# Down projection of 12 of 22 FFN pairs from seven block products, on one core of Trainium2

## The chip, the cores and the metric

One core of one Trainium2 chip runs the whole kernel; the other cores do nothing. The metric is device time in microseconds of one execution. TensorE multiplies matrices into PSUM; VectorE, ScalarE and GpSimd work element by element; SyncE, ScalarE and GpSimd issue transfers. Each engine runs its own instructions in order and waits for the others by semaphores.

## What is computed

An encoder block over 512 tokens of width 2048. The last part, which the change touches, is the channel mixing:

```python
h = modulate(layer_norm(x), shift2, scale2)
f = (jax.nn.silu(h @ w_ffn_gate[l]) * (h @ w_ffn_up[l])) @ w_ffn_down[l]
x = layer_norm_affine(DEEPNORM_ALPHA * x + gate2 * f, ln2_g[l], ln2_b[l])
```

The hidden width is 5632. All of it is float32.

## The kernel before

**Splits.** A float32 matrix is held as a high part (a cast to fp32r by ScalarE, line 95) and a low part (the rest, a subtraction by VectorE, line 96). `mm3` (lines 76 to 79) makes one float32 product out of three matmuls: high by high, high by low, low by high. So each product costs three matmuls, and each weight block needs one cast and one subtraction first. Split weights sit in four buffers each, `wh` and `wl`; raw weights in four buffers `raw` of 1024 elements by 128 partitions (512 KB).

**Pairs.** The hidden width is worked in 22 pairs of 256 rows. For each pair the gate product, SiLU, the up product and their product (`eg`, line 1138) give the pair's hidden values, 128 partitions by four blocks of 256, and `store_hid` (line 1016) writes them to `hid_d` in device memory from ScalarE's queue. Pairs 0 and 1 are made plainly. For pairs 2 to 21 the gate and up products are already made from seven block products in place of eight (`strassen`): a loop of four units, each with one load of 512 KB, `weight_sums` (three sums by GpSimd into `tt`, lines 1058 to 1060, and two splits, `hr`/`lr` and `wh`/`wl`), and 42 matmuls of 256 columns. `combine` (lines 1088 to 1092) adds the banks up on ScalarE and VectorE.

**Down projection.** It follows all the pairs. `down` takes four pairs at a time (0 to 3, 4 to 7, and so on to 19). `load_hid` (lines 1105 to 1111) loads a pair's hidden values and splits them into tiles that stay for the group (`A`, `M`, at the end `hh`, `hl`). Then, for each of four column chunks of 512 and each pair: one weight load of 512 KB, one split, and 4 token tiles x 2 row blocks x 3 matmuls of 512 columns. After each chunk four banks are drained by VectorE: multiplied by the gate row (`gate2`, line 1158) and added to the residual (lines 1161, 1163). The residual and the gate row come in with the first group on ScalarE's queue (lines 1151, 1153). Pairs 20 and 21 come last, in one stage with the final layer norm; their weights are multiplied by `gate2` on GpSimd and split during the last group (`load_last`, lines 1205 to 1213).

**Order.** The order within each engine is set by a scheduler of the language, from dependencies and the buffers that are free; the program's text gives the priorities. PSUM has eight banks, `ps_s` (4), `ps_g` (2), `ps_t` (2).

## Time and profile before

| | |
|---|---|
| median of 3 runs | 2667.24 us (2667.1 to 2670.86) |
| the profiled execution's own time | 2664.01 us |
| its span | 2662.0 us |
| TensorE busy | 2592.6 us (97%), 15563 matmuls recorded |
| VectorE, ScalarE, GpSimd busy | 1833.2, 1012.9, 1206.8 us (69%, 38%, 45%) |
| moved by DMA | 456.11 MB, 171 GB/s on average |

The profile is one execution, 3.2 us below the median of the timed runs. The gate and up products of pairs 2 to 21 lie at about 1330 to 2172 us of the span, the down projection at 2172 to 2608, the last two pairs and the final layer norm from there to the end. An engine's share of the whole span is a mean over stages with different limits, so the rows further down are taken by stage.

### The profile page before, as it was taken

What the parts mean: (1) busy time and instruction counts of PE and PEld (TensorE: products, weight loads), DVE (VectorE), ACT (ScalarE), POOL (GpSimd) and SP (SyncE); (2) the same over time, 40 slices, a digit from 0 to 9 for tenths busy, and PEclk for the clock granted to TensorE, in tenths of its full rate; (3) what the DMA queues carried; (4) which work ended last, traced back from release to release, by engine and by line L of the source; (5) the groups of instructions that cost most, each with busy time, mean ns of one, the idle gap of its engine ahead of it and who ended that gap; (6) DMA issues with size and microseconds to landing.
All of it is one profiled execution on the core that took longest, in us unless ns stands there. A gap on an engine that the chain in (4) does not pass through costs nothing. (4 is left out here: it accounts for less than half of the span.)

```text
span 2662.0 us, 40015 instructions
## 1 busy us (share of the span) xinstructions
PE 2592.6 (97%) x15563; PEld 2314.5 (87%) x15563; DVE 1833.2 (69%) x2244; ACT 1012.9 (38%) x1456; POOL 1206.8 (45%) x1033
## 2 busy tenths in 40 slices
PE   5999999999989999999899999999999999999998
PEld 4888888789878888888899999999999998888886
DVE  8886787874678644577777677777777755445566
ACT  3332433333344533346644443444444432212321
POOL 0008778876745011020368777776677720000023
PEclk8999999999999999999999999999999999999999
DMA  9976578775734444768753333333333364334442
GB/s 350 320 256 211 156 228 254 244 246 173 237 101 151 129 144 142 240 217 260 238 166 120 118 120 119 115 120 124 111 120 123 116 214 150 119 110 128 151 127 87
DMA packets 330798, 456.11 MB, mean 171 GB/s; under 512 B 19656, under 2 KB 208480, under 8 KB 330096
## 3 DMA queue, kind: packets, MB, share of 16 engines
q1 hardware_dynamic: 307840, 414.77, 49.3%
q10 hardware_dynamic: 22768, 38.78, 4.1%
q8 instruction: 122, 2.00, 0.3%
q14 instruction: 68, 0.56, 0.1%
HBM read 418.87 MB, written 34.62 MB: 170 GB/s over the span
## 5 line engine op out<-in xcount | busy, mean ns | idle before, releaser
L96 DVE TENSOR_TENSOR wl<-raw,wh 128x1024 fp32r<-128x1024 f32 (+2 forms) x342 | 446.7, 1310 | 323.0 <-ACT wh L95 321.6
L95 ACT CAST wh<-raw 128x1024 fp32r<-128x1024 f32 (+2 forms) x342 | 346.3, 1015 | 706.9 <-PE ps_s L79 270.7
L96 DVE TENSOR_TENSOR wl<-tt,wh 128x1024 fp32r<-128x1024 f32 x160 | 235.7, 1474 | 168.3 <-ACT wh L95 168.1
L1058 POOL TENSOR_TENSOR tt<-raw 128x512 f32<-128x512 f32 x160 | 244.2, 1527 | 190.7 <-DMA raw<-in_w_ffn_up_dram 70.0
L95 ACT CAST wh<-tt 128x1024 fp32r<-128x1024 f32 x160 | 167.7, 1049 | 309.4 <-PE ps_s L78 134.5
L1056 DVE TENSOR_TENSOR lr<-raw,hr 128x768 fp32r<-128x768 f32 x160 | 215.4, 1346 | 44.7 <-ACT hr L1055 44.0
L230 POOL TENSOR_TENSOR acc<-acc,tmp 128x512 f32<-128x512 f32 (+1 forms) x154 | 207.3, 1346 | 9.8
L1208 POOL TENSOR_TENSOR raw<-raw,gate 128x512 f32<-128x512 f32 x16 | 25.3, 1609 | 400.9 <-DMA raw<-in_w_ffn_down_dram 400.9
L1055 ACT CAST hr<-raw 128x768 fp32r<-128x768 f32 x160 | 133.6, 835 | 151.0 <-PE ps_s L78 71.4
L226 POOL TENSOR_SCALAR tmp<-braw,csil 128x512 f32<-128x512 f32 x112 | 136.3, 1218 | 117.8 <-DMA braw<-in_w_ada_dram 114.4
L1060 POOL TENSOR_TENSOR tt<-raw,tt 128x256 f32<-128x256 f32 x160 | 174.5, 1092 | 11.7
L1059 POOL TENSOR_TENSOR tt<-raw,tt 128x256 f32<-128x256 f32 x160 | 170.6, 1067 | 11.7
L77 PE MATMUL ps_g<-hTh,wh 128*128 128x512 f32 x384 | 152.1, 397 | 1.7 <-ACT wh L95 1.7
L79 PE MATMUL ps_g<-hTh,wl 128*128 128x512 f32 x384 | 151.0, 394 | 0.0
L78 PE MATMUL ps_g<-hTl,wh 128*128 128x512 f32 x384 | 150.4, 392 | 0.0
L220 DVE SCALAR_TENSOR_TENSOR acc<-braw,csil,acc 128x512 f32<-128x512 f32 x112 | 112.6, 1006 | 43.4 <-DMA braw<-in_w_ada_dram 42.5
L77 PE MATMUL ps_s<-wh,hTh 128*128 128x512 f32 (+1 forms) x384 | 138.1, 361 | 0.0
L77 PE MATMUL ps_s<-sh,wh 128*128 128x256 f32 x480 | 135.2, 282 | 2.7 <-ACT wh L95 2.7
L79 PE MATMUL ps_s<-sh,wl 128*128 128x256 f32 x480 | 136.2, 284 | 1.4 <-DVE wl L96 1.4
L78 PE MATMUL ps_s<-wl,hTh 128*128 128x512 f32 (+1 forms) x384 | 137.5, 358 | 0.0
L79 PE MATMUL ps_s<-wh,hTl 128*128 128x512 f32 (+1 forms) x384 | 137.2, 358 | 0.0
L78 PE MATMUL ps_s<-sl,wh 128*128 128x256 f32 x480 | 136.3, 284 | 0.0
(432 smaller groups left out, 8251.5 us busy)
## 6 DMA issues: line engine op xcount, KB each, us to landing
braw<-in_w_ada_dram SPq DMA_DIRECT2D x128, 512.0 KB, 4.3
raw<-in_w_in_dram SPq DMA_DIRECT2D x96, 512.0 KB, 5.0
raw<-in_w_ffn_gate_dram SPq DMA_DIRECT2D x96, 512.0 KB, 3.6
raw<-in_w_ffn_up_dram SPq DMA_DIRECT2D x96, 512.0 KB, 3.6
raw<-in_w_ffn_down_dram SPq DMA_DIRECT2D x88, 512.0 KB, 3.7
raw<-in_w_out_dram SPq DMA_DIRECT2D x64, 512.0 KB, 4.4
lraw<-in_w_ada_dram SPq DMA_DIRECT2D x56, 512.0 KB, 8.9
braw<-in_w_in_dram SPq DMA_DIRECT2D x24, 512.0 KB, 4.7
```

Source lines behind the costliest of these rows:

```text
L77: nc.tensor.matmul(ps, lhsT=ah, rhs=bh, start=start, stop=False)
L78: nc.tensor.matmul(ps, lhsT=ah, rhs=bl, start=False, stop=False)
L79: nc.tensor.matmul(ps, lhsT=al, rhs=bh, start=False, stop=stop)
L95: nc.scalar.copy(out=h[:, :n], in_=src)
L96: nc.vector.tensor_tensor(out=l[:, :n], in0=src, in1=h[:, :n], op=ALU.subtract)
L226: nc.gpsimd.tensor_scalar(out=dst[:, :n], in0=v[:, k, :], scalar1=col, scalar2=1.0, op0=ALU.mult, op1=ALU.mult)
L230: nc.gpsimd.tensor_tensor(out=acc2[:, :n], in0=acc2[:, :n], in1=dst[:, :n], op=ALU.add)
L1055: nc.scalar.copy(out=hr, in_=b[:, :, 1:4, :])
L1056: nc.vector.tensor_tensor(out=lr, in0=b[:, :, 1:4, :], in1=hr, op=ALU.subtract)
L1058: nc.gpsimd.tensor_tensor(out=t[:, :, 0:2, :], in0=b[:, :, 0:1, :].broadcast_to([P, 2, 2, P]), in1=b[:, :, 1:3, :], op=ALU.subtract)
L1059: nc.gpsimd.tensor_tensor(out=t[:, :, 2, :], in0=b[:, :, 2, :], in1=t[:, :, 0, :], op=ALU.subtract)
L1060: nc.gpsimd.tensor_tensor(out=t[:, :, 3, :], in0=b[:, :, 3, :], in1=t[:, :, 2, :], op=ALU.subtract)
```

## The change

Pairs 2 to 13 get their down projection from seven block products. Hidden values and weights are seen as 2 x 2 blocks (hidden: token halves by row blocks of the pair; weights: row blocks by halves of the 2048 columns).

- After the pair's product (line 1196 of the new file) `hidden_sums` makes four sums on GpSimd into `eu`. During the next pair's gate product the hook `pay` calls `store_parts` twice: it splits `eg` and `eu` (two more casts and subtractions of 1024) and stores the seven blocks that the products need, high and low, to `sets_d` from ScalarE's queue (line 1154), eight transfers of 0.13 or 0.26 MB a pair, 1.835 MB.
- The down projection of these 12 pairs is `strassen_down`: first three products for both column halves (`set1`, `weights1`), then four (`set2`, `weights2`). A unit is one pair and one column half: 18 or 24 matmuls of 512 columns. Weight sums are made on VectorE (lines 1174, 1175; 1226, 1227), then split as before. `need1` and `need2` (lines 1136, 1140) load the stored splits straight into a ring of 12 tiles, with no cast; `need2` of a pair is issued three units after its last use in the first set.
- Half tiles come by turns from `raw` (4) and `tp` (4 more). Sums stay in the accumulators `x2` without `gate2`; `convert` (lines 1268, 1269) multiplies by `gate2` and adds the residual, eight times, spread over the plain groups.
- Pairs 0, 1, 14 to 19 are done plainly in two groups of four, as before, 20 and 21 in the last stage. `load_last` multiplies in one GpSimd operation of 1024.

```diff
-    GROUP, N_LAST = 4, 2
+    GROUPS = [[2, 3, 4, 5, 6, 7, 8, 9, 10, 11, 12, 13]]
+    PLAIN = [[0, 1, 14, 15], [16, 17, 18, 19]]
+    N_LAST = 2
...
+    def need1(g):
+        tl = set1[g] = ring_tile((3, g))
+        nc.sync.dma_start(out=parts(tl).bitcast(F32)[:, :, 0:768], in_=sets_d[g][:, :, 1024:1792])
+
+    def need2(g):
+        tl = set2[g] = ring_tile((4, g))
+        nc.sync.dma_start(out=parts(tl).bitcast(F32), in_=sets_d[g][:, :, 0:1024])
+
+    def hidden_sums(g, eg, e):
+
+        nc.gpsimd.tensor_tensor(out=e[:, 0], in0=eg[:, 1], in1=eg[:, 2], op=ALU.subtract)
+        nc.gpsimd.tensor_tensor(out=e[:, 1], in0=e[:, 0], in1=eg[:, 3], op=ALU.subtract)
+        nc.gpsimd.tensor_tensor(out=e[:, 2], in0=eg[:, 3], in1=eg[:, 1], op=ALU.subtract)
+        nc.gpsimd.tensor_tensor(out=e[:, 3], in0=eg[:, 0], in1=e[:, 1], op=ALU.add)
+
+    def store_parts(g, v, moves):
+        for x, part in enumerate(split(v.rearrange("p b n -> p (b n)"), 1024)):
+            pb = part.bitcast(F32).rearrange("p (b n) -> p b n", b=4)
+            for to, b0, b1, st in moves:
+                n = (b1 - b0 + st - 1) // st
+                nc.scalar.dma_start(out=sets_d[g][:, x, to * 256:(to + n) * 256].rearrange("p (b n) -> p b n", b=n), in_=pb[:, b0:b1:st, :])
...
+    def weights1(g, c):
+        a, b = half_tile(), half_tile()
+        av, bv = a.rearrange("p (b n) -> p b n", b=2), b[:, :512]
+        nc.sync.dma_start(out=av, in_=w_rows(g, 0, c))
+        nc.sync.dma_start(out=bv, in_=w_rows(g, 1, c)[:, 1, :])
+        nc.vector.tensor_tensor(out=av[:, 1], in0=av[:, 1], in1=av[:, 0], op=ALU.add)
+        nc.vector.tensor_tensor(out=bv, in0=bv, in1=av[:, 1], op=ALU.add)
+        ah, al = split(a, 1024)
+        bh, bl = split(bv, 512)
+        return ((0, (ah[:, :512], al[:, :512])), (2, (bh[:, :512], bl[:, :512])), (1, (ah[:, 512:], al[:, 512:])))
...
-        bk = strassen(w_ffn_gate, 2 * g, "ssss")
+        bk = strassen(w_ffn_gate, 2 * g, "ssss", pay)
...
-        store_hid(g, eg)
...
+        if g in by_sums:
+            hidden_sums(g, eg, eu)
+            owed.append(lambda g=g, v=eg: store_parts(g, v, ((0, 0, 3, 2), (4, 3, 4, 1))))
+            owed.append(lambda g=g, v=eu: store_parts(g, v, ((2, 2, 4, 1), (5, 0, 2, 1))))
+        else:
+            store_hid(g, eg)
...
+    def weights2(g, c):
+        a, b = half_tile(), half_tile()
+        av, bv = a.rearrange("p (b n) -> p b n", b=2), b.rearrange("p (b n) -> p b n", b=2)
+        nc.sync.dma_start(out=bv, in_=w_rows(g, 0, c))
+        nc.sync.dma_start(out=av, in_=w_rows(g, 1, c))
+        nc.vector.tensor_tensor(out=bv, in0=bv, in1=av, op=ALU.add)
+        nc.vector.tensor_tensor(out=bv[:, 0], in0=bv[:, 0], in1=bv[:, 1], op=ALU.add)
+        ah, al = split(a, 1024)
+        bh, bl = split(b, 1024)
...
+    def products(pairs, sets, weights, c, step):
+        bk = None
+        for u, g in enumerate(pairs):
+            ws = ready.pop(0) if ready else weights(g, c)
+            if bk is None:
+                bk = [dbank() for _ in range(2 * len(ws))]
+            step(u, False)
+            for j, (b, w) in enumerate(ws):
+                for i in range(2):
+                    mm3(bk[2 * j + i], block(sets[g], b, i), w, u == 0, u == len(pairs) - 1)
+            step(u, True)
+        return bk
...
+    def convert(c, ts=range(NT)):
+        for t in ts:
+            zv = quad(x2[t], c)
+            xc = half_tile().rearrange("p (b n) -> p b n", b=2)
+            nc.sync.dma_start(out=xc, in_=quad(x2_d[t], c))
+            nc.vector.tensor_tensor(out=zv, in0=zv, in1=quad(gate2, c), op=ALU.mult)
+            nc.vector.scalar_tensor_tensor(out=zv, in0=xc, scalar=ALPHA, in1=zv, op0=ALU.mult, op1=ALU.add)
```

The order of the instructions changes at three places.

**ScalarE, end of an up product to the next gate product.** `eu<-ps_t` is the first step of the up product's `combine`; `hr` and `wh` are casts of the weights for the coming units. Before:

```order
L1088 COPY eu<-ps_t 128x256
L1055 CAST hr<-raw 128x768
L95 CAST wh<-tt 128x1024
L1055 CAST hr<-raw 128x768
L95 CAST wh<-tt 128x1024
L1016 DMA hid_d<-eg 128x1024
L1055 CAST hr<-raw 128x768
L95 CAST wh<-tt 128x1024
```

and now:

```order
L1089 COPY eu<-ps_t 128x256
L1056 CAST hr<-raw 128x768 x2
L95 CAST wh<-eg 128x1024
L95 CAST wh<-tt 128x1024
L1154 DMA sets_d<-wh 128x2x256
L1154 DMA sets_d<-wh 128x256
L1154 DMA sets_d<-wl 128x2x256
L1154 DMA sets_d<-wl 128x256
L95 CAST wh<-eu 128x1024
L1056 CAST hr<-raw 128x768
L1154 DMA sets_d<-wh 128x512 x2
L95 CAST wh<-tt 128x1024
```

The one store of `eg` gives way to two more casts and eight stores, and casts of weights stand between and behind these stores in the queue.

**SyncE, second half of the first product set** (before: the first group of the down projection). `raw` and `tp` are weight tiles; `Ah`, `Al` and their like are tiles of the ring, or before, of a group's hidden values. Before:

```order
L1108 DMA raw<-hid_d 128x1024 x2
L89 DMA raw<-in_w_ffn_down_dram 128x2x512 x16
L1108 DMA raw<-hid_d 128x1024 x4
L89 DMA raw<-in_w_ffn_down_dram 128x2x512 x16
L1108 DMA raw<-hid_d 128x1024 x4
```

and now:

```order
L1173 DMA raw<-in_w_ffn_down_dram 128x512
L1140 DMA Ah_23001<-sets_d 128x2x1024
L1172 DMA tp<-in_w_ffn_down_dram 128x2x512
L1140 DMA Al_23035<-sets_d 128x2x1024
L1173 DMA raw<-in_w_ffn_down_dram 128x512
L1172 DMA tp<-in_w_ffn_down_dram 128x2x512
L1173 DMA raw<-in_w_ffn_down_dram 128x512
L1140 DMA Ah_23069<-sets_d 128x2x1024
L1172 DMA tp<-in_w_ffn_down_dram 128x2x512
L1173 DMA raw<-in_w_ffn_down_dram 128x512
L1140 DMA Al_23103<-sets_d 128x2x1024
```

A weight load of 512 KB per 24 matmuls becomes two loads of 512 and 256 KB per 18, with one load of a pair's stored splits (line 1140) between them.

**VectorE, between the column halves of the second product set** (before: between two chunks of a group). `ps_g`, `ps_t`, `ps_s` are banks that are drained, `x_0` to `x_3` the accumulators. Before:

```order
L96 TENSOR_TENSOR wl<-raw,wh 128x1024 x4
L1158 TENSOR_TENSOR dtmp<-ps_s,gate_22227 128x512 x2
L1163 TENSOR_TENSOR x_0_22220<-x_0_22220,dtmp 128x512
L1163 TENSOR_TENSOR x_1_22221<-x_1_22221,dtmp 128x512
L1158 TENSOR_TENSOR dtmp<-ps_s,gate_22227 128x512 x2
L1163 TENSOR_TENSOR x_2_22222<-x_2_22222,dtmp 128x512
L1163 TENSOR_TENSOR x_3_22223<-x_3_22223,dtmp 128x512
L96 TENSOR_TENSOR wl<-raw,wh 128x1024 x4
```

and now:

```order
L1226 TENSOR_TENSOR raw<-raw,tp 128x1024
L1261 TENSOR_TENSOR x_0_22467<-ps_g,x_0_22467 128x512
L96 TENSOR_TENSOR wl<-raw,wh 128x1024
L1261 TENSOR_TENSOR x_1_22468<-ps_g,x_1_22468 128x512
L1261 TENSOR_TENSOR x_0_22467<-ps_t,x_0_22467 128x512
L1227 TENSOR_TENSOR raw<-raw 128x512
L1261 TENSOR_TENSOR x_1_22468<-ps_t,x_1_22468 128x512
L1261 TENSOR_TENSOR x_2_22469<-ps_s,x_2_22469 128x512
L1324 TENSOR_TENSOR x_2_22469<-x_2_22469,ps_s 128x512
L96 TENSOR_TENSOR wl<-tp,wh 128x1024
L1261 TENSOR_TENSOR x_3_22470<-ps_s,x_3_22470 128x512
L1324 TENSOR_TENSOR x_3_22470<-x_3_22470,ps_s 128x512
```

Four drains of two operations and a split of weights per unit become drains of one operation each, between the sums (lines 1226, 1227) and two splits of every unit; multiplications by `gate2` (line 1268) follow at once.

## Rows read from the trace of the kernel before

**Rows 1.** The page: busy shares of the span, and the granted TensorE clock in 40 slices.

```profile
PE 2592.6 (97%) x15563; PEld 2314.5 (87%) x15563; DVE 1833.2 (69%) x2244; ACT 1012.9 (38%) x1456; POOL 1206.8 (45%) x1033
...
PEclk8999999999999999999999999999999999999999
```

**Rows 2.** Windows: busy us of PE, PEld, DVE, ACT, POOL; clock, DMA share, GB/s.

```profile
1400.00:2100.00 700.00, 699.11 (x5831) 698.72 (x5831) 503.16 (x439) 289.49 (x331) 516.92 (x423) 1.00 0.38 119
2180.00:2280.00 100.00, 100.00 (x442) 82.78 (x442) 48.67 (x59) 23.73 (x23) 0.00 (x0) 1.00 0.53 170
2280.00:2380.00 100.00, 100.00 (x443) 82.81 (x442) 48.43 (x59) 23.85 (x23) 0.00 (x0) 1.00 0.38 120
...
2480.00:2580.00 100.00, 100.00 (x443) 82.81 (x442) 63.53 (x70) 33.41 (x38) 22.03 (x14) 1.00 0.50 159
```

**Rows 3.** TensorE in order of time, down projection: start us, us, line, operation.

```profile
2214.72 0.39 PE L79 MATMUL ps_t<-wh,Al 128*128 128x512 f32 x1
2214.95 0.39 PE L77 MATMUL ps_t<-wh,Ah 128*128 128x512 f32 x1
2215.17 0.39 PE L78 MATMUL ps_t<-wl,Ah 128*128 128x512 f32 x1
...
2217.44 0.39 PE L79 MATMUL ps_s<-wh,Al 128*128 128x512 f32 x1
```

**Rows 4.** VectorE in order of time, and its costliest group, down projection.

```profile
2586.11 0.67 DVE L1163 TENSOR_TENSOR x<-x,dtmp 128x512 f32<-128x512 f32 x1
2586.71 0.68 DVE L1211 TENSOR_TENSOR Ml<-raw,Mh 128x512 fp32r<-128x512 f32 x1
...
2589.71 1.21 DVE L96 TENSOR_TENSOR wl<-raw,wh 128x1024 fp32r<-128x1024 f32 x1
2590.84 0.68 DVE L1163 TENSOR_TENSOR x<-x,dtmp 128x512 f32<-128x512 f32 x1
...
L96 DVE TENSOR_TENSOR wl<-raw,wh 128x1024 fp32r<-128x1024 f32 x56 | 68.3, 1222 | 117.8 <-ACT wh L95 117.8
```

**Rows 5.** Windows with busy DMA queues, same columns.

```profile
20.00:40.00 20.00, 8.31 (x47) 6.84 (x46) 19.39 (x42) 8.60 (x14) 1.13 (x2) 0.77 1.08 365
40.00:60.00 20.00, 18.29 (x78) 14.98 (x76) 19.86 (x31) 5.99 (x7) 0.00 (x0) 0.89 1.07 371
...
1100.00:1130.00 30.00, 30.00 (x134) 24.85 (x133) 16.89 (x17) 11.69 (x12) 0.00 (x0) 1.00 0.75 246
2174.00:2200.00 26.00, 26.00 (x117) 21.52 (x116) 10.62 (x14) 5.55 (x6) 0.00 (x0) 1.00 0.95 329
```

**Rows 6.** ScalarE's queue at the start of the down projection; hidden stores (ns min/median/max).

```profile
2179.09 3.21 ACTq L1153 DMA_DIRECT2D x<-x_d  x3
...
2184.31 1.05 ACT L95 CAST wh<-raw 128x1024 fp32r<-128x1024 f32 x1 [8.20 <-DMA x<-x_d]
...
L1016 ACTq DMA_DIRECT2D hid_d<-eg x17: 326/326/388, 1534.6 to 2182.4; - x17
```

**Rows 7.** Gate and up stage, groups by line, 1500 to 2100 us: count, busy us, mean ns.

```profile
L96 DVE TENSOR_TENSOR wl<-tt,wh 128x1024 fp32r<-128x1024 f32 x120 | 179.2, 1493 | 126.4 <-ACT wh L95 126.4
...
L95 ACT CAST wh<-tt 128x1024 fp32r<-128x1024 f32 x119 | 124.9, 1049 | 223.2 <-PE ps_s L78 117.9 <-PE ps_t L78 100.5 <-POOL tt L1058 2.3
...
L1060 POOL TENSOR_TENSOR tt<-raw,tt 128x256 f32<-128x256 f32 x120 | 131.2, 1093 | 9.4
L1059 POOL TENSOR_TENSOR tt<-raw,tt 128x256 f32<-128x256 f32 x119 | 122.3, 1028 | 9.3
```

More of the change, by code (lines that the diff above doesn't have):

```diff
@@ new lines, in ring_tile, with vacate, half_tile, parts @@
+    def ring_tile(who, dt=F32R):
+        n = vacant.pop(0)
+        held[who] = n
+        pool, tag = RING[n]
+        return pool.tile([P, 4, 512], dt, tag=tag, name=tag)
+    def vacate(who):
+        vacant.append(held.pop(who))
+    extra_tiles = []
+    RAW_ONLY = 6
+    def half_tile():
+        place[1] += 1
+        if extra_tiles and place[1] > RAW_ONLY and place[1] % 2:
+            return extra_tiles[0].tile([P, 1024], F32, tag="tp", name="tp", bufs=4)
+        return raw_tile()
+    def parts(tl):
+        return tl.rearrange("p (x a) n -> p x (a n)", x=2)
@@ new lines, in block_kernel, with early @@
+    first = GROUPS[0]
+    ready = []
+    def early(u):
+        need1(first[u])
+        if u == 2:
+            ready.extend(weights1(first[v], 0) for v in range(2))
+    for g in range(N_SPLIT, N_PAIR):
+        eg = etile()
+        bk = strassen(w_ffn_gate, 2 * g, "ssss", pay)
+        combine(eg, bk)
+        nc.scalar.activation(out=eg, in_=eg, func=AF.Silu)
+        bk = strassen(w_ffn_up, 2 * g, "ggtt", early if g == N_PAIR - 1 else None)
+        eu = sw.tile([P, 4, 256], F32, tag="eu", name="eu", bufs=1)
+        combine(eu, bk)
+        nc.vector.tensor_tensor(out=eg, in0=eg, in1=eu, op=ALU.mult)
+        if g in by_sums:
[4 more added lines that the diff above has]
+            store_hid(g, eg)
@@ L1165, in block_kernel, with down @@
[L1165 to L1173 removed]
+        plain_hid[g] = Hid(h, l)
+    def down(pairs, cols, following, todo):
+        following = list(following)
+        for n, cc in enumerate(cols):
+            cs = slice(cc * 512, (cc + 1) * 512)
             bb = [dbank() for _ in range(NT)]
[L1175 to L1178 removed]
+            for u, g in enumerate(pairs):
+                hl = load_split(w_ffn_down, g * 256, 2, cc * 512, 512)
@@ L1179, in down @@
                 for t in range(NT):
                     for k in range(2):
-                        mm3(bb[t], hid[u].at(k, t), pair(hl, slice(None), k), u == 0 and k == 0, u == n - 1 and k == 1)
-            if extra is not None:
-                extra(cc)
-            for t in range(NT):
-                drain(bb[t], t, cc, first_)
-    g0 = 0
-    for gi in range(4):
-        hid = first_hid if gi == 0 else [load_hid(g0 + i, *hid_slot(4 * (gi % 2) + i)) for i in range(GROUP)]
-        down(g0, hid, gi == 0)
-        g0 += GROUP
@@ L1192, in block_kernel @@
-    pop("sw", "left")
-    hp = push("hp", "left")
-    def hp_hid(g):
-        return load_hid(g, hp.tile([P, 4, 256], F32R, tag="hh", name="hh", bufs=6), hp.tile([P, 4, 256], F32R, tag="hl", name="hl", bufs=6))
+                        mm3(bb[t], plain_hid[g].at(k, t), pair(hl, slice(None), k), u == 0 and k == 0, u == len(pairs) - 1 and k == 1)
+                if todo:
+                    todo.pop(0)()
+                if n == 3:
+                    vacate((0, g))
+                tick(following.pop(0) if following and n == 3 else None)
@@ new lines, in block_kernel @@
+    for gi in range(len(GROUPS)):
+        if gi + 1 < len(GROUPS):
+            left = strassen_down(gi, [lambda g=g: need1(g) for g in GROUPS[gi + 1]])
+            assert not left
+        else:
+            spare = len(RING) - len(GROUPS[gi])
+            for f in queue[:spare]:
+                tick(f)
+            queue = strassen_down(gi, queue[spare:])
+    if PLAIN:
+        todo = [lambda c=c, t=t: convert(c, [t]) for c in range(2) for t in range(NT)]
+        for grp in PLAIN:
+            queue = down(grp, (0, 2, 1, 3), queue, todo)
@@ L1221, in block_kernel @@
+    while later:
+        f = later.pop(0)
+        if f is not None:
+            f()
+    for f in queue:
+        f()
+    if not PLAIN:
+        convert(1)
     for t in range(NT):
```

206 lines of the change are left out of this document (133 added, 73 removed).

## The prediction

> **What bounds the kernel now.** I read the page's busy shares first: TensorE is busy 97% of the span at a granted clock of nine tenths or more in every slice after the first [rows 1]. So any time saved has to be TensorE time, unless the change makes TensorE wait. Then I took the two stages that the change touches by windows [rows 2]. In the gate and up products TensorE is busy 699.1 of 700 us, with 5831 matmuls recorded, 0.120 us each. In the down projection it is busy for all of every 100 us, with 442 to 443 matmuls, and the granted clock is 1.00 (the 2.4 GHz level) in both. The view of TensorE's waits from 1500 us to the end names none. The reader is to see that nothing else ends last there: VectorE is busy 72% and 48 to 64%, ScalarE 41% and 24 to 33%, GpSimd 74% in the first stage and idle in most of the second. Last, TensorE's order of time in the down projection: 2214.72 to 2217.44 is twelve starts, 0.2267 us each [rows 3]; "0.39" is the length of one in the pipeline, not its price.
>
> **The change, part by part.**
>
> *Matmuls removed.* One pair's down projection was 4 column chunks x 4 token tiles x 2 x 3 = 96 matmuls of 512 columns. By seven products it is 7 x 2 column halves x 2 token tiles x 3 = 84, of the same shape. Twelve pairs save 144 (the order counts 15333 and 15189 on TensorE). 144 x 0.2267 = **32.65 us**, all on the path, since TensorE waits for nothing there. The Trainium skill ("TensorE: Matmul & The Clock Gate", section Back-to-back issue gap) gives about 131 ns as the sustained spacing at 512 columns and 518 cycles as the isolated gap; by the first the saving would be an estimated 18.9 us, by the second some 31. The row agrees with the second, not the first, and the row stands.
>
> *The new stage itself* is 12 x 84 = 1008 matmuls, 228.5 us of TensorE. It is 24 units of 18 matmuls (three products, 4.08 us) and 24 of 24 (four products, 5.44 us). What must run beside them:
>
> VectorE. The timeline gives 0.60 us from start to start for 512 elements and 1.13 for 1024 [rows 4]. A unit of 18 has two adds of 512 and splits of 1024 and 512: 0.60 x 3 + 1.13 = 2.93 us, 72% of the unit. A unit of 24 has an add of 1024, one of 512 and two splits of 1024: 3 x 1.13 + 0.60 = 3.99 us, 73%. ScalarE has casts of 1.05 and half of it, 1.6 us, or of 2 x 1.05 = 2.1 [rows 7]. In the last twelve units VectorE also gets nine splits of reloaded hidden pairs and four multiplications (13 x 1.13 = 14.7 us) and ten bank drains (6 us): 47.9 + 20.7 = 68.6 us against 65.3 of TensorE. That is over 100% at its tightest, cushioned only by weights split up to two units ahead and by an order that puts the matmuls that need only high parts first. I put 1 us on it; the bound above is the 3.3 us of excess and 2 of slips, 5.
>
> DMA. A pair now moves 2 x 786 KB and 2 x 1049 KB of weights and 786 + 1049 KB of stored splits: 5.51 MB, with gate2 67.1 MB in 228.5 us, 294 GB/s. The rows with full queues show 365 and 371 GB/s, the start of the down projection 329 on average [rows 5]. The tightest place is the second half of the first product set, where 786 KB of weights and up to 1049 KB of splits fall in each 4.08 us: 450 GB/s for about nine units. At 370 GB/s the shortfall is 9 x (1.835 - 1.51) = 2.9 MB, 8 us, about what four half tiles of lead (two units and more) hide; at 350 it is 3.7 MB, some 10.5 us, and 2 to 3 us come through; at 330, 5 us; at 300, 10 us. I take 2 us (0 to 10), nearest the rows with full queues.
>
> *Work taken out of the down projection.* For 12 pairs the reload and its split go, and most drains lose their multiplication. VectorE waits for others half the time there [rows 2], so this is worth nothing. Nor is a gain to be had from the sixteen residual loads on ScalarE's queue, though one cast waited 8.20 us behind them [rows 6]: TensorE did not wait meanwhile.
>
> *Added to the gate and up products.* For each of the 12 pairs: four GpSimd sums of 128x256, two casts and two subtractions of 1024, and eight DMA issues in place of one, all within about three units (15.1 us; a unit is 42 x 0.120 = 5.04) after the pair's product. By the rows of that stage [rows 7] the subtractions are 2 x 1.49 = 3.0 us, the casts 2.1, the sums 4 x 1.03 to 1.09 = 4.2; the issues are 8 x 0.33 = 2.6 us of ScalarE if like the hidden store's 0.33 to 0.39, and 8 x 1.07 = 8.6 if like the crowded ones (3.21 for three) [rows 6]. VectorE is idle 28% of three units, 4.2 us, so a margin of 1.2; GpSimd is idle 26%, 3.9 us, 0.3 short, which spills into the fourth unit; ScalarE is idle 59%, 8.9 us. ScalarE's idle time before the casts is ended by TensorE 218 of 223 us, by GpSimd 2.3 [rows 7]: the casts wait for buffers that TensorE must free, so preparation runs ahead by its buffers. I cost this at **nothing**; the cover is that lead. Walked through the new order with these durations, no sum or split is ready less than 1.2 us before TensorE is due at it. If the cover goes, 1 to 1.5 us per pair show, 12 to 18 us. The bound below is nothing.
>
> One rule speaks against this part. A split's subtraction takes 1.493 us here, beside GpSimd busy 74%, and 1.222 in the down projection without it [rows 4, 7]. The Trainium skill ("GPSIMD Engine Reference", section Key points) says that GpSimd shares its SBUF interfaces with VectorE and contends with instructions that have two SBUF inputs; the trace agrees. By the rows, 0.27 / 1.22 at 74% is 30% beside a GpSimd that never rests, so 4.2 us more of it cost VectorE at most 4.2 - 4.2 / 1.30 = 1.0 us a pair, out of the margin of 1.2: the cover thins to 0.2 us and just holds.
>
> *The end.* The plain groups, the last two pairs and the final layer norm hold the same matmuls; what is left of the conversions (multiply by gate2, add the residual) is 12 x 1.13 = 14 us of VectorE, spread over the 8 x 96 x 0.2267 = 174 us of the plain pairs, in which it is at most 64% busy [rows 2]: nothing.
>
> **Sum.** The profiled execution took 2664.01 us. 2664.0 - 32.65 + 1 + 2 + 0 = 2634.4. The median of the runs is 2667.24, 3.2 above it; I add that: **2637 us**. With no stall at all it is 2634.6.
>
> **Rivals.**
>
> (a) *DMA backlog.* For it: 294 GB/s for 228 us is more than any stage but the first holds, and the start of the down projection held 329. Against: rates of 365 to 371 are seen, and after the peak the second set asks only 1049 KB per 5.44 us, 193 GB/s. At 330 to 300 GB/s it shows 5 to 10 us: 2640 to 2645.
>
> (b) *Gate and up stage late.* The cover above fails by 1 to 1.5 us per pair: 2634.6 + 12 to 18 = 2647 to 2653. For it: GpSimd's and VectorE's thin margins, and casts that stand behind DMA issues in ScalarE's queue, some of which wait for a subtraction. Against: the lead of the buffers.
>
> (c) *VectorE and ScalarE in series.* If adds, casts and subtractions of a unit follow each other instead of overlapping across units, a unit of 24 costs 3.99 + 2.10 = 6.09 and one of 18 costs 2.93 + 1.60 = 4.53 us: 24 x (0.65 + 0.45) = 26 us back, 2661; with the extras of the last twelve units, 2665. That is 6 us faster to 2 us faster, on either side of 0.2%.
>
> (d) *Slower: the load rate of mixed traffic.* The stage breaks even when 67.1 MB take 261.2 us, at 257 GB/s; below 252 the kernel is slower by over 0.2%. In one stretch [rows 5] the queues moved 246 GB/s at a share of 0.75. If the mixture holds there (weight rows in pieces of 2 KB, loads of splits that wait on SyncE's queue for a tile that TensorE must release, weights queued behind them), the stage takes 67.1 / 0.246 = 272.8 us, and the run 2667.2 - 261.2 + 272.8 = 2678.8. Against it: a share of 0.75 is demand, not a ceiling.
>
> That the change removes less than it says is no rival here: the order counts 144 matmuls fewer, all of the one shape.
>
> **How the numbers follow.** A measurement of this kernel tells about 0.2%, 5.3 us, from no change. My forecast, stalls of 0 to 5 us (2634.6 to 2640), has 0.54; (a) 0.14; (b) 0.17; (c) 0.10, half of it within 0.2%; (d) 0.05. So faster 0.54 + 0.14 + 0.17 + 0.05 = 0.90, same 0.05, slower 0.05. The range reaches from 2632, the pure saving with a run's scatter, to 2653, the end of (b); (c) and (d) are left out.
>
> **What would show it.** Right: in the new stage TensorE starts at 0.2267 us, over 440 matmuls in 100 us, with VectorE about 75% and no wait over 1 us; the gate and up stage keeps 0.120 us each. Wrong by (a): TensorE waits in the last units of the first set's second half for a cast that itself waits for a weight load. By (b): a wait of 1 us or more, twelve times, for wl or wh within three units of an up product's end. By (c): VectorE over 90% in the second set with TensorE waiting for wl throughout. The forecast fails if the new stage holds under 420 matmuls in 100 us.

## The result, and the profile after

The change makes the kernel **slower**: 2686.88 us median (2682.14 to 2687.97, 4 runs) against 2668.52 us before (2667.1 to 2670.86, 4 runs), a ratio of 1.0064 with a 95% interval of 1.0052 to 1.0076. The profiled execution took 2682.14 us, its span is 2680.3 us against 2662.0.

The page after (busy shares, granted clock in 40 slices), beside [rows 1]:

```profile
PE 2587.1 (97%) x15419; PEld 2304.9 (86%) x15419; DVE 1957.2 (73%) x2340; ACT 1054.2 (39%) x1516; POOL 1279.7 (48%) x1073
...
PEclk8999999999999999999999999999999999999999
```

TensorE is busy for less time, as it should with 144 matmuls less, and yet the span is longer. Where it went is seen from the first matmul of the down projection, in TensorE's order of time:

```profile
2216.68 0.28 PE L79 MATMUL ps_t<-Mh,wl 128*128 128x256 f32 x1
2216.80 0.40 PE L77 MATMUL ps_s<-wh,Ah 128*128 128x512 f32 x1
```

In the trace before it starts at 2172.08 us. Both stages begin level: the first matmul of `sh` by `hr` in pair 2's gate product starts at 1364.97 before and 1365.33 after. So the gate and up products took 807.1 us before and 851.5 now, **44.4 us more**. From there to the start of the last matmul it is 478.5 us before (2650.60) and 452.1 after (2668.92), **26.4 us less**. 44.4 - 26.4 and 0.3 ahead make the 18.3 us between the spans. These two lengths, "the stage" and "down projection and end", are what the experiments are read by; the stage is counted from that matmul, some 4.7 us later than in the expectations of the first runs.

The windows after, columns as in [rows 2]:

```profile
1500.00:1600.00 100.00, 95.36 (x766) 94.72 (x765) 74.22 (x62) 41.96 (x50) 81.27 (x64) 0.97 0.46 148
1700.00:1800.00 100.00, 94.46 (x758) 93.39 (x757) 71.58 (x61) 40.56 (x48) 81.18 (x66) 0.97 0.42 132
2000.00:2100.00 100.00, 100.00 (x837) 100.00 (x836) 70.59 (x63) 41.18 (x47) 70.36 (x60) 1.00 0.37 117
2280.00:2320.00 40.00, 40.00 (x178) 33.14 (x177) 28.10 (x36) 16.27 (x21) 0.00 (x0) 1.00 1.04 396
...
2400.00:2440.00 40.00, 38.95 (x171) 31.59 (x170) 38.35 (x38) 21.24 (x22) 0.00 (x0) 1.00 0.82 281
2520.00:2560.00 40.00, 40.00 (x178) 33.13 (x177) 24.35 (x26) 11.18 (x11) 2.87 (x1) 1.00 0.39 128
```

While the 12 pairs are worked, TensorE starts 758 to 766 matmuls in 100 us, not 837, and its granted clock is 0.97; from 2000 us, when no pair has parts to store, it is back at 837. In the down projection it starts 178 in 40 us, the old pace, but 171 near the end of the second product set. The queues moved 396 GB/s for 40 us in the first set's second half, at no cost to TensorE.

TensorE's waits (total us, times, longest), first up to 2200 us, then behind:

```profile
PE ps_t L79 <- DVE lr L1057: 22.0, 12, 2.2
...
PE ps_s L78 <- DVE wl L96: 1.6, 2, 1.0
PE ps_s L77 <- ACT wh L95: 0.6, 1, 0.6
PE ps_g L77 <- DVE x L1261: 0.3, 1, 0.3
```

Twelve waits, one a pair, each for `lr`, the low part of a weight split on VectorE, in the last unit of the up product (`ps_t`). They sum to 22.0 us. The rest lies mostly in matmuls that ran at the lower clock. TensorE in order of time at one of the waits, and windows of 3 us around it:

```profile
1530.57 0.39 PE L77 MATMUL ps_t<-Mh,hr 128*128 128x256 f32 x1 [0.52 <-ACT hr L1056]
...
1533.30 0.48 PE L79 MATMUL ps_t<-Mh,lr 128*128 128x256 f32 x1 [2.23 <-DVE lr L1057]
1533.58 0.42 PE L77 MATMUL ps_t<-Mh,hr 128*128 128x256 f32 x1
1533.80 0.41 PE L78 MATMUL ps_t<-Ml,hr 128*128 128x256 f32 x1
```

```profile
1528.00:1531.00 3.00, 2.48 (x20) 2.15 (x18) 2.60 (x2) 2.52 (x3) 1.76 (x3) 1.00 0.02 6
1531.00:1534.00 3.00, 0.77 (x4) 0.70 (x4) 2.25 (x2) 0.00 (x0) 3.00 (x2) 0.91 0.00 0
1534.00:1537.00 3.00, 3.00 (x16) 3.00 (x16) 0.82 (x1) 1.90 (x3) 2.50 (x4) 0.52 0.56 175
1537.00:1540.00 3.00, 3.00 (x27) 3.00 (x27) 3.00 (x3) 0.89 (x2) 2.19 (x2) 1.00 0.07 18
```

After a wait of 2.23 us the matmuls of 256 columns start 0.213 us apart, not 0.120, and the granted clock is 0.52 (the 1.2 GHz level) where it was 1.00. The starts stay that far apart for 17 matmuls, 3.64 us: 17 x 0.094 = 1.6 us lost beside the wait. 2.1 + 1.6 = 3.7 us, and twelve times that is 44 us. The parts differ from pair to pair: nine of the twelve waits, of 1.89 to 2.23 us, were followed by 14 to 27 slow matmuls, those of 0.74 and 0.84 us and one of 1.94 by none to speak of. Added up over the stage from the distances of the starts, 26.2 of the 44.4 us lie at waits and 17.1 in slow matmuls.

That is where the time lies, not what makes it. The period from one pair's product (line 1196) to the next is 40.2 us before and 43.85 to 43.96 here, in all eleven steps between the twelve pairs, with slow matmuls or without. One pair without:

```profile
1709.01 0.39 PE L79 MATMUL ps_t<-Mh,lr 128*128 128x256 f32 x1 [1.94 <-DVE lr L1057]
1709.23 0.28 PE L77 MATMUL ps_t<-Mh,hr 128*128 128x256 f32 x1
1709.35 0.28 PE L78 MATMUL ps_t<-Ml,hr 128*128 128x256 f32 x1
```

The starts are 0.12 us apart again at once, and still the next pair's wait for `lr` ends 43.91 us later. The product starts 9.79 to 9.84 us behind the end of that wait in eleven pairs, whether slow matmuls lie between or not. So the fall of the clock adds nothing to the 3.7 us: what TensorE does not lose at the lower clock it loses in the next waits. The round of a pair is set by the engines that prepare its weights.

Why `lr` is late is read backwards. VectorE, then ScalarE, in order of time:

```profile
1507.21 1.23 DVE L96 TENSOR_TENSOR wl<-eu,wh 128x1024 fp32r<-128x1024 f32 x1 [2.53 <-ACT wh L95]
...
1527.93 1.49 DVE L96 TENSOR_TENSOR wl<-tt,wh 128x1024 fp32r<-128x1024 f32 x1 [1.90 <-ACT wh L95]
1529.82 2.03 DVE L96 TENSOR_TENSOR wl<-tt,wh 128x1024 fp32r<-128x1024 f32 x1 [0.41 <-ACT wh L95]
1531.78 1.47 DVE L1057 TENSOR_TENSOR lr<-raw,hr 128x768 fp32r<-128x768 f32 x1
```

```profile
1506.13 1.05 ACT L95 CAST wh<-eu 128x1024 fp32r<-128x1024 f32 x1 [3.64 <-POOL eu L1147]
...
1526.85 1.05 ACT L95 CAST wh<-tt 128x1024 fp32r<-128x1024 f32 x1 [5.38 <-POOL tt L1061]
...
1529.69 0.83 ACT L1056 CAST hr<-raw 128x768 fp32r<-128x768 f32 x1
```

The cast that this `lr` needs, the one at 1529.69, was done at 1530.52 us, and TensorE had waited for it too: its first matmul by that `hr` starts at 1530.57. The cast needs only a raw weight, which GpSimd had begun to read at 1521.12. But it stands in ScalarE's queue behind the SiLU and two casts of `tt`, the first of which waited 5.38 us for GpSimd. Its subtraction then stands 1.3 us behind one of `wl` in VectorE's queue. So the split is late on both engines because GpSimd's `tt` is late. And GpSimd, at the pair's product:

```profile
1497.30 0.74 POOL L1061 TENSOR_TENSOR tt<-raw,tt 128x256 f32<-128x256 f32 x1
1500.54 1.39 POOL L1144 TENSOR_TENSOR eu<-eg 128x256 f32<-128x256 f32 x1 [2.49 <-DVE eg L1196]
1501.88 1.71 POOL L1146 TENSOR_TENSOR eu<-eg 128x256 f32<-128x256 f32 x1
1503.56 1.72 POOL L1145 TENSOR_TENSOR eu<-eu,eg 128x256 f32<-128x256 f32 x1
1505.36 0.74 POOL L1147 TENSOR_TENSOR eu<-eg,eu 128x256 f32<-128x256 f32 x1
1506.05 1.29 POOL L1059 TENSOR_TENSOR tt<-raw 128x512 f32<-128x512 f32 x1
...
1511.60 2.34 POOL L1059 TENSOR_TENSOR tt<-raw 128x512 f32<-128x512 f32 x1 [1.16 <-DVE wl L96]
```

GpSimd was idle 2.49 us: the first hidden sum stands in its queue and waits for the product. Then the four sums take 5.5 us, and only at 1506.05 does it come to the weight sums of the next up product's first unit. Behind the sums stand their cast (ScalarE idle 3.64 us before it) and their subtraction (VectorE idle 2.53 us), and behind those the next weights. There the round closes: the `tt` that GpSimd had finished at 1498.04 is cast only at 1508.91, behind the cast of the sums, its subtraction ends at 1511.52, and only then can GpSimd write `tt` again, at 1511.60. GpSimd's waits and groups from 1500 to 1900 us, after; then its waits before:

```profile
POOL tt L1059 <- DVE wl L96: 45.6, 35, 1.7
POOL eu L1144 <- DVE eg L1196: 25.0, 10, 2.5
...
L1059 POOL TENSOR_TENSOR tt<-raw 128x512 f32<-128x512 f32 x72 | 127.0, 1769 | 47.4 <-DVE wl L96 45.6 <-DMA raw<-in_w_ffn_gate_dram 1.8
...
L1145 POOL TENSOR_TENSOR eu<-eu,eg 128x256 f32<-128x256 f32 x10 | 17.2, 1719 | 0.0
```

```profile
POOL tt L1058 <- DMA raw<-in_w_ffn_up_dram: 38.1, 20, 3.1
POOL tt L1058 <- DMA raw<-in_w_ffn_gate_dram: 38.1, 18, 3.8
POOL tt L1058 <- DVE wl L96: 26.7, 23, 1.2
```

Before, GpSimd waited for data, 76.2 us in 400: that was its slack, 7.6 us a pair. After, it never waits for data but 1.8 us: a pair costs it 5.6 us of sums and 2.5 of standing for the product, its own weight sums are longer (the first 1.77 us in place of 1.49, all three of eight units 30.4 us a pair in place of 28.8, by the means), and it waits longer for VectorE to give back `tt` (45.6 in place of 26.7).

### The profile page after: what moved, and what is told of

Its sections match the earlier page's. It is cut to its first block, busy times and chain, and to the rows that moved or that the text cites. A ratio compares the mean times of both kernels' runs of the same rounds, so it can differ in the third digit from the quotient of the medians.

```text
span 2680.3 us, 40177 instructions
## 1 busy us (share of the span) xinstructions
PE 2587.1 (97%) x15419; PEld 2304.9 (86%) x15419; DVE 1957.2 (73%) x2340; ACT 1054.2 (39%) x1516; POOL 1279.7 (48%) x1073
## 4 chain that ended last, share of the span: by engine, by line
PE 24%; POOL 13%; DVE 7%; issue 3%; ACT 2%; DMA 2%; POOLq 0%; ACTq 0%; DVEq 0%; SPq 0%
POOL tt L1059 5%; PE ps_s L78 4%; PE ps_s L79 4%; PE ps_s L77 4%; POOL tt L1060 3%; PE ps_g L77 2%; PE ps_g L78 2%; PE ps_g L79 2%; DVE wl L96 2%; PE ps_t L79 2%; PE ps_t L77 2%; PE ps_t L78 2%; POOL tt L1061 2%; DVE lr L1057 2%; ACT wh L95 1%
## 5 line engine op out<-in xcount | busy, mean ns | idle before, releaser
L96 DVE TENSOR_TENSOR wl<-raw,wh 128x1024 fp32r<-128x1024 f32 (+2 forms) x345 | 440.9, 1282 | 229.5 <-ACT wh L95 227.7
L95 ACT CAST wh<-raw 128x1024 fp32r<-128x1024 f32 (+2 forms) x345 | 338.8, 985 | 634.1 <-PE ps_s L79 216.2
L96 DVE TENSOR_TENSOR wl<-tt,wh 128x1024 fp32r<-128x1024 f32 x160 | 248.8, 1555 | 164.5 <-ACT wh L95 163.8
L1059 POOL TENSOR_TENSOR tt<-raw 128x512 f32<-128x512 f32 x160 | 267.8, 1678 | 127.2 <-DVE wl L96 83.5
L1057 DVE TENSOR_TENSOR lr<-raw,hr 128x768 fp32r<-128x768 f32 x160 | 227.4, 1432 | 18.4 <-ACT hr L1056 18.2
L1060 POOL TENSOR_TENSOR tt<-raw,tt 128x256 f32<-128x256 f32 x160 | 187.8, 1178 | 8.2
L1061 POOL TENSOR_TENSOR tt<-raw,tt 128x256 f32<-128x256 f32 x160 | 146.1, 917 | 8.2
L1376 POOL TENSOR_TENSOR tp<-tp,gate 128x1024 f32<-128x1024 f32 x5 | 15.0, 3015 | 272.5 <-DMA tp<-in_w_ffn_down_dram 272.5
L78 PE MATMUL ps_g<-sl,wh 128*128 128x256 f32 x480 | 138.2, 288 | 0.0
L79 PE MATMUL ps_g<-sh,wl 128*128 128x256 f32 x480 | 137.6, 287 | 0.0
L77 PE MATMUL ps_g<-sh,wh 128*128 128x256 f32 x480 | 137.3, 286 | 0.0
```

The lines of the kernel that those rows point to most:

```text
L77: nc.tensor.matmul(ps, lhsT=ah, rhs=bh, start=start, stop=False)
L78: nc.tensor.matmul(ps, lhsT=ah, rhs=bl, start=False, stop=False)
L79: nc.tensor.matmul(ps, lhsT=al, rhs=bh, start=False, stop=stop)
L95: nc.scalar.copy(out=h[:, :n], in_=src)
L96: nc.vector.tensor_tensor(out=l[:, :n], in0=src, in1=h[:, :n], op=ALU.subtract)
L1057: nc.vector.tensor_tensor(out=lr, in0=b[:, :, 1:4, :], in1=hr, op=ALU.subtract)
```

## The experiments

In the first runs one part at a time is taken out or put in. "Stage" and "down projection and end" come from each run's trace. A time without a count is that of a single run. Beside them, the kernel before took 2663 to 2672 us in its own runs, and the stage took 808.5 to 809.2 us in the three traces whose gate and up products are the same (sums on VectorE, and the two tries at the down projection).

**Sums on VectorE.**

```diff
-        nc.gpsimd.tensor_tensor(out=e[:, 0], in0=eg[:, 1], in1=eg[:, 2], op=ALU.subtract)
+        nc.vector.tensor_tensor(out=e[:, 0], in0=eg[:, 1], in1=eg[:, 2], op=ALU.subtract)
```

(and so for all four)

> The changed kernel with the four hidden sums of each pair on VectorE in place of GpSimd. Theory G (the 5.5 us that the four sums hold GpSimd put its weight sums late, and everything behind them; 44 us of the gate and up stage come from there): the stage from the first gate product of pair 2 to the start of the down projection goes back from 856 us to 812 to 822, VectorE taking 4 x 0.4 us more a pair; the kernel takes 2643 to 2653. Rival S (ScalarE's eight stores and the buffers that they hold make the stage late): no change, 2685 to 2689. Rival V (VectorE's added work makes the stage late): worse, 2690 to 2705.

2640.36 us (4 runs), ratio to the kernel before 0.9908, interval 0.988 to 0.9936: **faster than both**. Stage 808.6 us, down projection and end 451.4. Windows of 1500 to 1900 us:

```profile
1500.00:1900.00 400.00, 399.78 (x3336) 399.58 (x3335) 324.07 (x304) 177.39 (x209) 327.34 (x242) 1.00 0.48 150
```

VectorE is 81% busy and TensorE waits 0.2 us of 400. Rivals S and V fall as sole causes: all stores and splits are still there, and VectorE has more to do than in the change.

**No sums.**

```diff
-            hidden_sums(g, eg, eu)
```

The second split and its stores take the up product in place of the sums, so the down projection of the 12 pairs gives something else.

> The changed kernel with the four hidden sums left out, so that the second split and its stores take the up product in place of the sums; the down projection of the 12 pairs then gives something else. Theory G: the stage is back at 812 to 816 us, the kernel at 2640 to 2646. Rival S: 2685 to 2689, nothing moves. Rival V: in between or as rival S, since both splits stay on VectorE.

2651.05 us, stage 816.6, down projection and end 451.7. Most of the loss goes, not all: 9.5 us stay with less work than the run above, which has the sums and loses 1.5. Neither theory said that; the order of VectorE's instructions differs between the two, and why this one keeps 9.5 us stays open.

**What the gate and up products got, with the plain down projection.** Into the kernel before go `hidden_sums`, `store_parts`, `pay` and their calls for pairs 2 to 13; `hid_d` is stored and read as before.

> The kernel before with only what the change adds to the gate and up products (sums, splits, stores of 12 pairs); the down projection stays as before and doesn't read the stored parts. All three theories: the stage takes 44 us more, the kernel 2708 to 2716. If a part of the 44 us came from elsewhere (order of the down projection's first loads, say), the stage takes less more and the kernel stays under 2700.

2708.71 us, stage 848.9, down projection and end 478.52, to the hundredth what it was before. So the loss is made wholly in the gate and up products, by what was added to them.

**The same without stores.**

```diff
-                nc.scalar.dma_start(out=sets_d[g][:, x, to * 256:(to + n) * 256].rearrange("p (b n) -> p b n", b=n), in_=pb[:, b0:b1:st, :])
+                pass
```

> The run before with sums and splits alone, without the eight stores of a pair from ScalarE's queue (nothing reads the parts). Theory G: the stage still takes 36 to 44 us more than before, the kernel 2704 to 2714. Rival S: the stage is back within 5 us of before, the kernel at 2667 to 2674. Rival V: as theory G.

2687.87 us, stage 825.6. Neither theory: 18.5 us stay without stores, 23 go. TensorE's waits for `lr` fall from 22.1 to 15.9 us with a longest of 1.6, and the granted clock over 1500 to 1900 us is 1.00 (0.98 with stores). The period is 41.77 us, with hardly a slow matmul.

**The sums alone.** Only `hidden_sums` goes into the kernel before, with no split of the sums and no store.

> The kernel before with the four GpSimd sums of 12 pairs alone: no split of them, no stores, and the plain down projection. Theory K (the loss needs the whole chain: product, sums, their cast and split standing in ScalarE's and VectorE's queues ahead of the next weights): stage 807 to 814 us, the kernel 2667 to 2675. Theory G1 (GpSimd's queue alone, 30.3 us of weight sums and 5.6 of these and the standing for the product): period about 41 to 41.5, stage 818 to 826 us, the kernel 2678 to 2687.

2669.28 us, stage 808.5: as theory K had it. Windows of 1500 to 1900 us:

```profile
1500.00:1900.00 400.00, 400.00 (x3340) 400.00 (x3339) 282.47 (x250) 164.41 (x189) 366.85 (x281) 1.00 0.38 119
```

GpSimd is 92% busy, and TensorE misses nothing. So the sums' time is not the loss. But two things differ here from the change: no split or store waits behind the sums, and the order puts the sums behind the weight sums of two more units, so that GpSimd never stands for the product. Which of the two covers them this run does not tell.

**The sums and both splits one unit later.** The hook gives out the sums in the first unit of the next gate product and the two splits in the second and third, in place of the first and second.

```diff
-            hidden_sums(g, eg, eu)
+            owed.append(lambda g=g, e=eg, v=eu: hidden_sums(g, e, v))
...
-        if u < 2 and owed:
+        if u < 3 and owed:
```

> The changed kernel with the four sums of a pair still on GpSimd, but given out one hook earlier than the splits, inside the next gate product: in GpSimd's queue they stand one unit later (behind the weight sums of the next up product's first unit in place of ahead of them), and VectorE's order alternates the two kinds of weight splits. Theory G1 (GpSimd's queue is full: 30.3 us of weight sums, 5.6 of hidden sums, 5.1 of waiting for VectorE and 2.5 of standing for the product make the 43.9 us of a pair): only the 2.5 us of standing go, the period falls to about 41.0 to 41.5 us, the stage to 818 to 824 us, the kernel to 2653 to 2660. Rival G2 (the time of the sums itself must come out of every pair, wherever they stand): period 43 to 44, kernel 2680 to 2687. Rival P (only their place and VectorE's order count): period 40.3, kernel 2640 to 2645.

2653.11 us, stage 821.1, period mostly 41.1: theory G1's numbers. The windows, and GpSimd's waits:

```profile
1500.00:1900.00 400.00, 394.63 (x3253) 390.58 (x3252) 308.45 (x261) 173.73 (x204) 371.40 (x272) 1.00 0.47 148
...
POOL tt L1059 <- DVE wl L96: 12.8, 11, 1.2
POOL tt L1059 <- DMA raw<-in_w_ffn_gate_dram: 4.5, 3, 1.8
```

GpSimd no longer stands for the product, and it waits 12.8 us for VectorE in place of 45.6; it is 93% busy. One unit's shift of sums and splits gives back 30 of 44 us, with all of them, and the stores, made on the same engines. The next run has a part of this shift alone.

**The sums' split later.**

```diff
-        if u < 2 and owed:
+        if u in (0, 2) and owed:
```

> The changed kernel, sums on GpSimd and eight stores as they are, with the second split of a pair (that of the sums) given out two units later in the next gate product. Theory K (the loss needs the chain in which the sums' cast and subtraction stand in ScalarE's and VectorE's queues ahead of weights that TensorE needs next): with those behind two units' weights, most of the loss goes: stage 808 to 822 us against 851 and 807 before, the kernel 2640 to 2655. Theory G1 (GpSimd's time alone): stage 845 to 852, the kernel 2680 to 2687.

2670.48 us (10 runs), ratio to before 1.0007, interval 0.9997 to 1.0016; stage 838.1. The split of the sums, moved one unit by itself, gives back 13 us: theory K overrated it. The other 17 of the 30 us above go to the sums and the first split, which no run tells apart. The sums still stand ahead of the up product's weight sums in GpSimd's queue here, and GpSimd stands 1.2 us for the product in place of 2.5.

**The sums twice.** The call of `hidden_sums` stands twice.

> The changed kernel with the four sums of each pair made twice on GpSimd (the same values). Theory G1: a full queue gets 5.6 us more per pair: period about 49.4 us, stage some 66 us longer, the kernel 2745 to 2757. If GpSimd isn't what paces the pair, part of it hides: under 2720.

2709.8 us, stage 875.6, period 46.0. 5.6 us more of sums a pair would be 49.4; 2.1 came. The scheduler had put the second half of the sums between the next weight sums. GpSimd's time alone does not set the period; the place of the sums in its queue does too. TensorE waits elsewhere in this run: 40.9 us for `wh` (ScalarE), not for `lr`.

**The stores' share**, three runs on the kernel before with all extras (stage 848.9, without stores 825.6): four stores a pair; low parts written in place, so that stores hold no low buffer; eight stores of an eighth of the columns.

```diff
-            owed.append(lambda g=g, v=eg: store_parts(g, v, ((0, 0, 3, 2), (4, 3, 4, 1))))
-            owed.append(lambda g=g, v=eu: store_parts(g, v, ((2, 2, 4, 1), (5, 0, 2, 1))))
+            owed.append(lambda g=g, v=eg: store_parts(g, v, ((0, 0, 4, 1),)))
+            owed.append(lambda g=g, v=eu: store_parts(g, v, ((4, 0, 4, 1),)))
```

> The kernel before with sums, splits and stores of 12 pairs and the plain down projection, with each split half stored in one transfer of four blocks in place of two: four stores a pair, not eight (2.10 MB, not 1.84). The stores cost 23 us of the stage in the run with eight. Theory Q (the issues on ScalarE's queue, 0.33 to 0.8 us each, hold up casts): about half comes back, stage 835 to 842 us, the kernel 2694 to 2702. Theory B (the bytes, or the buffers held until the stores have landed): stage 847 to 852, the kernel 2706 to 2712.

```diff
-        for x, part in enumerate(split(v.rearrange("p b n -> p (b n)"), 1024)):
+        src = v.rearrange("p b n -> p (b n)")
+        high = stream.tile([P, 1024], F32R, tag="wh", name="wh", bufs=4)
+        nc.scalar.copy(out=high, in_=src)
+        nc.vector.tensor_tensor(out=src, in0=src, in1=high, op=ALU.subtract)
+        for x, part in enumerate((high.bitcast(F32), src)):
```

> The kernel before with sums, splits and eight stores of 12 pairs and the plain down projection, with the low parts of the hidden values written over the values themselves instead of into the weights' low buffers, so that the stores hold no low buffer. Without stores the stage took 826 us, with them 849. Theory B (buffers held by stores): half or more comes back, stage 830 to 840 us, the kernel 2690 to 2700. Rival O (held buffers don't matter; the order that the stores give or the traffic does): 846 to 851, the kernel 2705 to 2711.

```diff
-                nc.scalar.dma_start(out=sets_d[g][:, x, to * 256:(to + n) * 256].rearrange("p (b n) -> p b n", b=n), in_=pb[:, b0:b1:st, :])
+                nc.scalar.dma_start(out=sets_d[g][:, x, to * 256:(to + n) * 256].rearrange("p (b n) -> p b n", b=n)[:, :, 0:32], in_=pb[:, b0:b1:st, 0:32])
```

> The kernel before with sums, splits and eight stores of 12 pairs and the plain down projection, each store cut to one eighth of its columns (nothing reads them): VectorE's order is the same, the number of issues too, the bytes 0.23 MB a pair in place of 1.84. Theory T (the traffic of the stores is what takes the stage from 826 us without stores to 849): stage 824 to 832, the kernel 2685 to 2692. Rival O (the order of the engines' instructions with the stores in it, and the falls of the clock that follow): 845 to 851, the kernel 2704 to 2711.

2711.69, 2711.6 and 2706.77 us; stages 850.2, 848.2 and 845.2. Neither the number of issues nor held low buffers nor (but for some 4 us) the bytes make it. What is left is that stores hold high buffers (`wh`), that they stand in ScalarE's queue and wait there for VectorE's subtraction, and the order that the scheduler makes around them; none of these was isolated.

**The down projection's missing 6 us.** The saving there should have been 32.65 us and is 26.4. Two tries, both on the run with sums on VectorE: a weight add on GpSimd, and the reloads at half the rate.

```diff
-        nc.vector.tensor_tensor(out=bv, in0=bv, in1=av, op=ALU.add)
+        (nc.gpsimd if c else nc.vector).tensor_tensor(out=bv, in0=bv, in1=av, op=ALU.add)
```

> The hidden sums on VectorE, and in the second half of the second product set the first weight add (1024 elements) on GpSimd, which is idle there. Theory D (of the 5.5 us that the down projection lacks against the pure saving, some 3 are lost there because VectorE is over 90% busy): VectorE falls from over 90% to about 75% there, waits of TensorE there go, down projection and end take 448 to 449 us in place of 451.4; the kernel takes 2636 to 2639. Rival: GpSimd's slower adds (about 3 us of 1024) or its contention with VectorE bring new waits; 2640 to 2646.

```diff
-                    tick(following.pop(0) if following and c == 1 else None)
+                    tick(following.pop(0) if following and c == 1 and u % 2 else None)
...
-                tick(following.pop(0) if following and n == 3 else None)
+                tick(following.pop(0) if following and (n == 3 or len(vacant) > sum(f is not None for f in later)) else None)
```

> The hidden sums on VectorE, and the reloads of the plain pairs' hidden values (a load, a cast, a subtraction of 1024 each) given out at half the rate in the last twelve units of the second product set, the rest during the plain groups. Theory D (VectorE is what TensorE waits for in those units): some five subtractions less there, 5.6 us of VectorE; the three us lost there come back, down projection and end take 448 to 449.5 us in place of 451.4, the kernel 2634 to 2639. Rival (the stops there come from the casts or from the order at the bank changes, not from VectorE's load): 451 to 452, the kernel as the run with sums on VectorE, 2638 to 2643.

2655.97 us (ratio to before 0.9946, 0.9929 to 0.9963) and 2647.44 (0.9927, 0.9912 to 0.9942), down projection and end 468.3 and 454.1 us in place of 451.4: both worse. Theory D is not settled by this, because neither edit took load off VectorE where it was meant to. The second column half of the second set, in the run with sums on VectorE and then with the reloads spread:

```profile
2340.60:2408.10 67.50, 66.85 (x289) 53.54 (x288) 65.93 (x68) 33.06 (x33) 4.04 (x1) 1.00 0.77 256
2345.10:2413.80 68.70, 66.07 (x290) 53.68 (x288) 64.26 (x66) 33.60 (x34) 0.00 (x0) 1.00 0.75 247
```

VectorE is busy 98% and 94%: nine splits of reloaded values fall there in place of ten, not five fewer. With the weight add on GpSimd its busy time in that half even rises, to 74.86 us of 82.40. VectorE and then GpSimd in that run, in order of time:

```profile
2397.95 0.69 DVE L1227 TENSOR_TENSOR tp<-tp 128x512 f32<-128x512 f32 x1 [2.30 <-POOL tp L1226]
2398.56 1.22 DVE L96 TENSOR_TENSOR wl<-tp,wh 128x1024 fp32r<-128x1024 f32 x1
2399.70 3.42 DVE L96 TENSOR_TENSOR wl<-raw,wh 128x1024 fp32r<-128x1024 f32 x1
```

```profile
2394.72 3.20 POOL L1226 TENSOR_TENSOR tp<-tp,raw 128x1024 f32<-128x1024 f32 x1 [3.02 <-DMA raw<-in_w_ffn_down_dram]
2399.62 2.43 POOL L1226 TENSOR_TENSOR raw<-raw,tp 128x1024 f32<-128x1024 f32 x1 [1.70 <-DMA tp<-in_w_ffn_down_dram]
```

VectorE's next add waits 2.30 us for GpSimd's, and a subtraction that takes 1.22 us takes 3.42 beside a GpSimd add of 2.43.

**Eighteen pairs**, with the sums on VectorE.

```diff
-    GROUPS = [[2, 3, 4, 5, 6, 7, 8, 9, 10, 11, 12, 13]]
-    PLAIN = [[0, 1, 14, 15], [16, 17, 18, 19]]
+    GROUPS = [[2, 3, 4, 5, 6, 7, 8, 9, 10, 11, 12, 13], [14, 15, 16, 17, 18, 19]]
+    PLAIN = [[0, 1]]
```

> The hidden sums on VectorE, and 18 pairs in place of 12 by seven products: pairs 2 to 13 in one group, 14 to 19 in a second, pairs 0 and 1 plainly. 6 x 12 = 72 matmuls less, 16.3 us. If the gate and up stage stays covered for 18 pairs as it was for 12, and the second group's drains (GpSimd adds, VectorE) and loads hide as the first group's did: 2624 to 2630. If the second group brings stops of its own (bank changes with longer drains, loads of the first set at its start): 2630 to 2640. If the drains on GpSimd and VectorE don't hide: over 2640.

With two pairs in the plain group, the conversion of two token tiles falls behind the first drains, so a part of their sum is multiplied by `gate2` twice; the operations are the same in number. 2652.89 us, ratio 0.9943, 0.9926 to 0.9960. The stage holds for 18 pairs (808.1 us). Down projection and end take 464.9 us, where the run with 12 pairs less 16.3 us would give 435.1: 29.8 us are lost anew. TensorE's waits there:

```profile
PE ps_g L78 <- DVE wl L96: 8.0, 6, 2.5
PE ps_s L77 <- DVE x L1261: 3.6, 1, 3.6
```

The bank changes of the second group come with VectorE behind, and waits of up to 3.6 us bring the clock down too (0.79 granted from 2535 to 2555 us).

## Why the prediction was wrong

- **Right.** The removed matmuls and their price: 0.2267 us is the pace in the new stage too (178 in 40 us). The down projection alone, by the forecast 29.65 us shorter, became 26.4 us shorter. The 2 us for DMA did not come: none of TensorE's waits there is put down to a load. DMA does not bind: rivals (a) and (d) name a ceiling that the 396 GB/s of one window refute. Rival (c) did not come: VectorE and ScalarE overlap across units.
- **The step that failed: "I cost this at nothing; the cover is that lead."** It cost 44.4 us, and with the plain down projection the same parts cost 41.8 (848.9 - 807.1). It was rival (b), with chance 0.17, and its price of 12 to 18 us was too small by a factor of about three. Its sign was near: twelve waits, ten of them over 1 us, but for `lr`, and 34 us behind the product, in the last unit of the next pair's up product. What the runs show in place of that step is this.
- *I counted GpSimd's sums as busy time, 4.2 us, and not as a place in a queue.* They took 5.5 us (1.39, 1.71, 1.72, 0.74), and the queue stood 2.5 us more for the product: 8.0 us in which the next up product's first weight sums could not be made. I compared each part with its own due time, "1.2 us" of margin for a single pass. The shift repeats in each pair, and what GpSimd gains on TensorE in eight units must pay it back; it doesn't. With the sums taken off GpSimd, 1.5 of the 44.4 us are left: that the loss needs the sums on GpSimd is shown. That their time alone is not enough is shown by the sums alone (1.4 us lost with GpSimd 92% busy). How the rest is shared is known in part: 13 us for the later split of the sums, 30 with the sums and the other split moved too, 23 for the stores; these shares overlap.
- *I took the lead of the buffers as cover for each engine by itself.* The engines close a round: GpSimd's `tt` waits for VectorE's subtraction, that for ScalarE's cast, and that cast stands behind the cast of the sums, which waits for GpSimd. `hr` and `lr`, which need only a raw weight, stand in the same queues behind work that waits for GpSimd, and come late with it. A round took 43.9 us, TensorE's work of a pair 40.2; the 3.7 us show as waits or as slow matmuls, and the sum is the same either way. So a price made of waits and, on top, of the clock would not be right either.
- **Mis-sized: stops in the down projection,** 1 us forecast for VectorE (the 2 for DMA did not come), 6.2 measured (32.65 - 26.4). Four starts come 0.6 to 1.4 us behind the one ahead, in place of 0.227: at 2230.39 (for a cast), 2383.59 (for a drain), 2416.48 and 2474.08 (for `wl`). The second comes right behind the change between the column halves of the second set, the third in the middle of its second half; at the change between the halves of the first set there is none. These four lose half of the 6.2 us, starts at 0.3 to 0.5 us most of the rest. In that second half VectorE was forecast at over 100% and was 96% busy, so it may well be the limit there, but my two attempts did not take its load down: the cause is open.
- **Contention** by the rule that I weighed was taken as at most 1.0 us a pair. VectorE's subtraction of `tt` went from 1.49 to 1.61 us, eight a pair, about that. But GpSimd lengthened too, which I had not priced: 1.6 us a pair on its weight sums and 1.4 on the hidden sums, together more than the standing. That VectorE's load makes these longer is not shown by a run of its own.

Left open: which property of the stores makes their 23 us, what keeps 9.5 us in the run without sums, and what stops TensorE in the down projection.

## What to carry to other kernels

Work added to an engine that is 74% busy is not priced by its busy time. Look at where it stands in the in-order queue, what it waits for there, and what stands behind it that the bound engine needs; if the delay comes back every round, add up the round through all the engines that hand work to each other, and compare it with the bound engine's time for a round. And before you add a fall of the clock to the price of a wait, compare the rounds that have it with the rounds that don't: here both took 43.9 us, so the slow matmuls used up time that would have been waited. The change itself was good: with the four sums on VectorE, which was busy for more of the time than before and let GpSimd wait 65.3 us in 400 but TensorE hardly at all, the kernel takes 2640.36 us, 0.9908 of the time before.
